# Grouped-query values: the low parts of the probabilities against the high parts of the values alone, in two column groups of 64

## The chip, the cores and the metric

The kernel runs on one core of one Trainium2 chip. The metric is the device time of one execution in microseconds (us), the median of several runs. The core has five engines with instruction queues of their own: TensorE (PE in the profile, with its weight loads apart as PEld), VectorE (DVE), ScalarE (ACT), GpSimd (POOL) and SyncE (SP, which here only issues DMAs).

## The reference, cut to what matters

Two layers of a transformer trunk on 512 latent and 256 context tokens of width 1024. Each layer has a neighbourhood attention and a grouped-query attention beside each other, which share one input projection. The change lies in the grouped-query attention of the latent queries: 8 query heads of width 64, two key/value heads (four query heads share one), 512 queries in four blocks of 128, 768 keys (256 context, 512 latent).

```python
def _attend(q, k, v):
    s = jnp.einsum('bqkgd,btkd->bkgqt', q, k).astype(jnp.float32) * (HEAD_DIM ** -0.5)
    p = jax.nn.softmax(s, axis=-1).astype(v.dtype)
    return jnp.einsum('bkgqt,btkd->bqkgd', p, v)
...
    k_all = jnp.concatenate([ckb, kb], axis=1)
    v_all = jnp.concatenate([cvb, vb], axis=1)
    b_att = _gqa_latent(qb, k_all, v_all)     # _attend for blocks of 128 queries
```

All of it is float32 in the reference.

## The kernel before

To keep float32 precision, the kernel splits operands into a high part and a low part (the rest after rounding), and sums products of the parts. In the projections that makes three matmuls out of one (`mm3`, lines 435 to 437). In the grouped-query attention, the probabilities of a head are turned (transposed) by DMA as two float16 halves: tile `ht` has 4 query blocks x 12 x 128 columns, where entries 0 to 5 of the 12 are the six key tiles of the high part, and 6 to 11 those of the low part (`turned`, lines 841 to 846). The values lie in tile `vb` as float16: for each key tile and key/value head 64 columns of high part beside 64 columns of low part.

`gq_values` (line 1167) computes the output of one head. `divide` first brings the reciprocals of the softmax sums to all partitions (four transposes, L853) and scales the gate `zb` with them (L854). Then 12 matmuls accumulate in one PSUM tile `po` of 128 partitions x 512 queries: for each of the six key tiles, the 128 columns of `vsl(k)` (high and low values) are the stationary operand, and all 512 queries of the probabilities' high part (L1178), then of the low part (L1179), are the moving one. So partitions 0 to 63 of `po` hold the product with the high values, 64 to 127 that with the low values, and `head_out` adds the two halves (L828 copies one on ScalarE, L829 adds the other on VectorE) and multiplies by the gate (L833 on GpSimd).

`pipeline` runs the scores of head h (`gq_scores`: L890 and L891 on PE, L1161 on DVE, the exponential L1162 on ACT, the two halves L841 on ACT and L842 on DVE or POOL, the turn L846) ahead of the values of head h-1, with projection work (`fill`: L435 to L437 on tiles `psf` and `psx`) handed in between. Layer 0 also has context queries (`ctx_scores`, `ctx_values`: L903, L905, L909, L925) and the weights' modulation sums (L297 on DVE, with tile `rawb` loaded by SP). The first projection of the kernel also uses matmuls with 32 stationary columns in four column groups (`ada_part`, L254).

The order of instructions on each engine is set when the kernel is built: a scheduler takes the instructions of all heads, estimates when each can run, and writes one fixed order for each engine. It places matmuls of the scores and of the fill between the matmuls of `gq_values` where it expects them to be ready. In some places the kernel fixes the order itself (`behind`).

Of the kernel before, what the change touches and what calls it, by code (L numbers as in the profile page):

```python
# [72 lines left out]
def hybrid_kernel(es: ExitStack, tc, x, ctx, cvec, w_ada, w_ada0, small, gvec, w_in, w_o_a, w_o_b, w_out,  # L73
                  bias_int, bias_edge, rope, ident_d, out):
    nc = tc.nc
    V, S, G, T = nc.vector, nc.scalar, nc.gpsimd, nc.tensor
# [39 lines left out]
    def psw(n=512, kind="w"):  # L116
        if kind == "w":
            kind = "f" if pm["i"] % pm["n"] == 0 else "x"
            pm["i"] += 1
            if pm["i"] in pm["v_for"]:  # L120
                kind = "v"
        pool, cols = pm[kind]
        return pool.tile([128, cols], F32, tag=kind, name=nm("ps" + kind))[:, :n]
# [471 lines left out]
    def layer(l, hx, nxt, start):  # L595
# [195 lines left out]
        if True:  # L791
# [29 lines left out]
            def head_out(po, e, dst, eng=None, back=None):  # L821

                n = dst.shape[-1]
                m, o = 64 * e, 64 * (1 - e)
                t1 = att["p"].tile([128, 512], F32, tag="ho", name=nm("ho"), bufs=1)
                a = t1[m:m + 64, :n]
                if back is None:
                    S.copy(a, po[o:o + 64, :n])  # L828
                    V.tensor_tensor(a, po[m:m + 64, :n], a, ALU.add)  # L829
                else:  # L830
                    S.activation(a, po[o:o + 64, :n], AF.Copy, scale=back[o:o + 64])
                    V.scalar_tensor_tensor(a, po[m:m + 64, :n], back[m:m + 64], a, ALU.mult, ALU.add)
                (eng or G).tensor_tensor(dst, dst, a, ALU.mult)  # L833
# [14 lines left out]
            def divide(ps, r, e, dst, back):  # L848

                n = r.shape[-1]  # L850
                V.reciprocal(r, r)
                for i in range(n):
                    T.transpose(ps[:, 128 * i:128 * i + 128], r[:, i:i + 1].to_broadcast([128, 128]), ident)  # L853
                V.scalar_tensor_tensor(dst, ps[64 * e:64 * e + 64, :128 * n], back[64 * e:64 * e + 64], dst,  # L854
                                       ALU.mult, ALU.mult)
# [227 lines left out]
            vb = vbig[:, 0:768].bitcast(F16).rearrange("p (t h q d) -> p t h q d", t=6, h=2, q=2)  # L1083
# [83 lines left out]
            def gq_values(h, st):  # L1167
                ht, r = st
                e, kv = h % 2, h // 4

                def vsl(t):
                    return vb[:, t, kv].rearrange("p q d -> p (q d)")
                dst = zb.rearrange("p (f n) -> p f n", f=4)[64 * e:64 * e + 64, h // 2, 0:512]
                divide(psw(512, "t"), r, e, dst, vs[:, 1:2])
                po = psw(512, "t")
                pv = po.rearrange("p (i n) -> p i n", i=4)
                for k in range(6):
                    T.matmul(pv, vsl(k), ht[:, :, k, :], start=k == 0, stop=False)  # L1178
                    T.matmul(pv, vsl(k), ht[:, :, 6 + k, :], start=False, stop=k == 5)  # L1179
                head_out(po, e, dst, V if h == 7 else G)  # L1180
                return vsl

# [12 lines left out]
            def early():  # L1195

                for c in (1, 3):
# [5 lines left out]
                   "junk": vbig[:, 2176:2432].bitcast(BF16)}  # L1203
            bg = gate_steps((1,), Parts(att["p"], own)) if first else []
            pipeline(fill, 8, gq_first, values_of(zb, gq_values, vs[:, 1:2], True), early, bg)
            gq_es.close()

# [322 lines left out]
```

## Time and profile before

| what | value |
|---|---|
| three runs | 1109.35, 1105.3, 1109.29 us |
| median | 1109.29 us |
| span of the profiled execution | 1109.3 us |
| PE busy | 1075.5 us, 97% of the span |
| PE weight loads busy | 879.1 us |
| DVE, ACT, POOL busy | 767.4, 617.1, 473.1 us |
| grouped-query stage of layer 0 | about 375 to 540 us of the span |
| grouped-query stage of layer 1 | about 946 to 1045 us of the span |

The profile shows one execution; its time is its span, since nothing else is shown around it. Busy time of an engine is the time in which at least one of its instructions ran. A matmul's shown duration includes its way through the array, so that several overlap; how fast matmuls follow one another is read from their starts. In the groups, a row gives line, engine, operation, output and inputs by the program's names, shapes and count, then the busy time and the mean duration in ns.

### The profile page before, as it was taken

The numbers are of one execution on the slowest core, as the hardware profiler recorded it, in microseconds if no ns is written. First come the engines' busy times: TensorE is split into PE (matmuls) and PEld (weight loads), VectorE is DVE, ScalarE is ACT, GpSimd is POOL, SyncE is SP. The second block draws the span as 40 slices with busy tenths as digits, with TensorE's granted clock in tenths as the row PEclk, the third lists the DMA queues.
The fourth block names the chain that finished last, engine by engine and source line by source line (L and its number), as shares of the span: only waits on it lengthen the run. The fifth ranks groups of instructions, "written<-read, shape, count | busy, mean of one in ns | idle before, by whom it ended". The sixth has DMA issues, their size and how long they took to land. (4 is left out here: it accounts for less than half of the span.)

```text
span 1109.3 us, 16937 instructions
## 1 busy us (share of the span) xinstructions
PE 1075.5 (97%) x5672; PEld 879.1 (79%) x5672; DVE 767.4 (69%) x1600; ACT 617.1 (56%) x1236; POOL 473.1 (43%) x397
## 2 busy tenths in 40 slices
PE   8999999999999989989999999999999999999998
PEld 5688888788888868767788878888877888777677
DVE  4667889975377487766777785366997665677473
ACT  6454279776433566765330275444899446786430
POOL 1054235555257154463621354232355472564531
PEclk9999999999999999998999999999999999999999
DMA  9455324554543379789633542453565536879642
GB/s 370 146 171 153 90 68 111 128 138 120 169 131 127 100 184 215 166 228 228 213 101 124 157 147 78 140 163 101 134 149 130 156 107 171 199 229 239 188 152 77
DMA packets 236000, 171.79 MB, mean 155 GB/s; under 512 B 160140, under 2 KB 201864, under 8 KB 234248
## 3 DMA queue, kind: packets, MB, share of 16 engines
q1 hardware_dynamic: 228576, 156.31, 51.6%
q0 software_dynamic: 2368, 7.87, 2.1%
q10 hardware_dynamic: 4968, 6.53, 1.8%
q8 instruction: 45, 0.74, 0.3%
q14 instruction: 43, 0.35, 0.1%
HBM read 115.58 MB, written 17.32 MB: 120 GB/s over the span
## 5 line engine op out<-in xcount | busy, mean ns | idle before, releaser
L842 POOL TENSOR_TENSOR h<-p,h 128x256 f16<-128x256 f32 (+2 forms) x104 | 113.6, 1101 | 160.0 <-ACT h L841 117.7
L422 POOL TENSOR_TENSOR wlo<-raw,whi 128x512 fp32r<-128x512 f32 x70 | 98.0, 1406 | 131.6 <-ACT whi L420 98.7
L435 PE MATMUL psf<-hx,whi 128*128 128x512 f32 (+1 forms) x360 | 138.2, 384 | 2.2 <-DVE zt L627 1.2
L436 PE MATMUL psf<-hx,whi 128*128 128x512 f32 (+1 forms) x360 | 136.1, 378 | 0.0
L437 PE MATMUL psf<-hx,wlo 128*128 128x512 f32 (+1 forms) x360 | 136.1, 378 | 0.0
L435 PE MATMUL psx<-whi,hx 128*128 128x512 f32 (+1 forms) x328 | 121.0, 372 | 0.0
L437 PE MATMUL psx<-whi,hx 128*128 128x512 f32 (+1 forms) x328 | 120.0, 367 | 0.0
L420 ACT CAST whi<-raw 128x512 fp32r<-128x512 f32 x136 | 83.2, 620 | 65.5 <-DMA raw<-in_w_in_dram 46.9
L436 PE MATMUL psx<-wlo,hx 128*128 128x512 f32 (+1 forms) x328 | 119.6, 366 | 0.0
L408 POOL TENSOR_TENSOR wlo<-raw,whi 128x512 fp32r<-128x512 f32 x40 | 59.8, 1499 | 117.7 <-ACT whi L405 74.6
L405 ACT CAST whi<-raw 128x512 fp32r<-128x512 f32 x88 | 54.3, 623 | 96.7 <-PE psx L437 34.2
L508 POOL TENSOR_TENSOR ss<-ss,ehalf 128x8 f32<-128x8 f32 (+2 forms) x40 | 63.6, 1593 | 77.2 <-DVE ss L505 72.2
L841 ACT CAST h<-p 128x256 f16<-128x256 f32 (+2 forms) x136 | 81.7, 616 | 5.3 <-DMA ht<-h 1.3
L422 DVE TENSOR_TENSOR wlo<-raw,whi 128x512 fp32r<-128x512 f32 x66 | 65.3, 992 | 25.9 <-ACT whi L420 24.3
L1161 DVE CUSTOM_DVE_ANT_0 p<-pss,vb 128x768 f32<-128x768 f32 x64 | 60.2, 953 | 31.0 <-PE pss L891 28.9
L1162 ACT ACTIVATE p<-pss,mx 128x768 f32<-128x768 f32 x64 | 57.6, 901 | 41.1 <-DVE mx L1161 40.4
L435 PEld LDWEIGHTS psf<-hx,whi 128*128 128x128 f32 x360 | 68.3, 190 | 14.9 <-ACT zt L625 1.9
L437 PEld LDWEIGHTS psf<-hx,wlo 128*128 128x128 f32 x360 | 68.2, 190 | 12.0
L436 PEld LDWEIGHTS psf<-hx,whi 128*128 128x128 f32 x360 | 68.3, 190 | 10.9
L437 PEld LDWEIGHTS psx<-whi,hx 128*128 128x128 f32 x328 | 61.9, 189 | 10.2
L436 PEld LDWEIGHTS psx<-wlo,hx 128*128 128x128 f32 x328 | 62.0, 189 | 9.5
L435 PEld LDWEIGHTS psx<-whi,hx 128*128 128x128 f32 x328 | 61.8, 189 | 9.1 <-issue 0.2
(338 smaller groups left out, 2984.7 us busy)
## 6 DMA issues: line engine op xcount, KB each, us to landing
raw<-in_w_in_dram SPq DMA_DIRECT2D x168, 256.0 KB, 3.0
rawb<-in_w_ada_dram SPq DMA_DIRECT2D x48, 256.0 KB, 2.8
raw<-in_w_out_dram SPq DMA_DIRECT2D x32, 256.0 KB, 2.9
tg<-gs SPq DMA_DIRECT2D x4, 1536.0 KB, 9.9
rawx<-in_w_ada_dram SPq DMA_DIRECT2D x4, 1024.0 KB, 10.3
rawy<-in_w_ada_dram SPq DMA_DIRECT2D x4, 1024.0 KB, 10.3
gs<-zt ACTq DMA_DIRECT2D x16, 256.0 KB, 2.6
raw<-in_w_o_a_dram SPq DMA_DIRECT2D x16, 256.0 KB, 3.1
```

Source lines behind the costliest of these rows:

```text
L405: S.copy(hi[:, :n], raw[:, :n])
L408: e.tensor_tensor(lo[:, :n], raw[:, :n], F(hi[:, :n]), ALU.subtract)
L420: S.copy(hi, raw)
L422: lo_eng(i).tensor_tensor(lo, raw, F(hi), ALU.subtract)
L435: T.matmul(ps, lhs[0], rhs[0], start=first, stop=False)
L436: T.matmul(ps, lhs[0], rhs[1], start=False, stop=False)
L437: T.matmul(ps, lhs[1], rhs[0], start=False, stop=last)
L508: G.tensor_tensor(ss, ss, ehalf[:, :n], ALU.pow)
L841: S.copy(h[:, 0], p[:, :n])
L842: eng.tensor_tensor(h[:, 1], p[:, :n], h[:, 0], ALU.subtract)
L1161: V.tensor_tensor_reduce(p, pss, lift, -1.0, 3e38, ALU.add, ALU.min, mx[:, 0:1])
L1162: S.activation(p, pss, AF.Exp, bias=mx[:, 0:1], accum_out=r[:, i:i + 1])
```

## The change

The high part of the probabilities is multiplied as before, but all six key tiles first. The low part is multiplied by the high values alone (64 stationary columns, `vhi(k)`), and in two matmuls instead of one: the first two query blocks (c = 0) write partitions 0 to 63 of `po`, the other two (c = 1) partitions 64 to 127. Since `head_out` adds the two halves of the partitions for every query, each query receives its low product once. The product of low probabilities and low values is no longer computed.

```diff
+
+                def vhi(t):
+                    return vb[:, t, kv, 0, :]
...
                 for k in range(6):
                     T.matmul(pv, vsl(k), ht[:, :, k, :], start=k == 0, stop=False)
-                    T.matmul(pv, vsl(k), ht[:, :, 6 + k, :], start=False, stop=k == 5)
+                for k in range(6):
+                    for c in range(2):
+                        T.matmul(pv[64 * c:64 * c + 64, 2 * c:2 * c + 2, :], vhi(k), ht[:, 2 * c:2 * c + 2, 6 + k, :],
+                                 start=False, stop=k == 5)
```

In the changed kernel L1181 is the high part (L1178 before) and L1184 the low part (L1179 before); lines 1180 and later have moved down by 6, so that DVE, ACT and POOL keep the lines used here up to 1162.

The scheduler writes another order from the first grouped-query head on. On PE, in the first head's values of layer 0, a score block of the next head (tile `pss`) stands between two products with `vb`. Before:

```order
L1178 MATMUL pst_4512<-ht_4208,vb_3419 128x512
L890 MATMUL pss_4458<-gk_3421,qs_4423 128x512
L891 MATMUL pss_4458<-gk_3421,qs_4423 128x512
L890 MATMUL pss_4458<-gk_3421,qs_4423 128x256
L891 MATMUL pss_4458<-gk_3421,qs_4423 128x256
L1179 LDWEIGHTS vb_3419
L1179 MATMUL pst_4512<-ht_4208,vb_3419 128x512
```

The same place on PE now, where a row of the low part has 64 stationary columns and 256 queries (64x256):

```order
L1181 MATMUL pst_4512<-ht_4208,vb_3419 128x512
L1184 LDWEIGHTS vb_3419
L1184 MATMUL pst_4512<-ht_4208,vb_3419 64x256
L890 MATMUL pss_4458<-gk_3421,qs_4423 128x512
L891 MATMUL pss_4458<-gk_3421,qs_4423 128x512
L890 MATMUL pss_4458<-gk_3421,qs_4423 128x256
L891 MATMUL pss_4458<-gk_3421,qs_4423 128x256
```

The score block has kept its place, and now stands behind the first of the twelve matmuls of the low part, which it parts from the other eleven. Counted over the whole order, the 192 matmuls of the low part stand in 27 unbroken runs. By head, in layer 0: 1+2+9, 4+3+5, 4+5+3, 12, 8+4, 7+3+2, 12, 12; in layer 1: 12, 12, 1+3+8, 12, 12, 12, 12, 12.

On DVE, some rows later in the same head: the reciprocal of the softmax sums (L851), the context scores' maximum (L903, L905), a low half (L842), a modulation sum (L297) and the next head's queries (L884). Before:

```order
L903 TENSOR_REDUCE mx_4494<-pss_4489 128x2
L842 TENSOR_TENSOR h_4467<-p_4463,h_4467 128x768
L297 ISA rawb_4455,asum<-rawb_4455,vb_3419 128x512
L297 ISA asum 128x1
L851 RECIPROCAL r_868_4427<-r_868_4427 128x4
L905 TENSOR_SCALAR mx_4494<-mx_4494 128x2
L884 TENSOR_TENSOR qs_4932<-qb_3734,qs_4932 64x768
```

And now:

```order
L903 TENSOR_REDUCE mx_4494<-pss_4489 128x2
L851 RECIPROCAL r_868_4427<-r_868_4427 128x4
L905 TENSOR_SCALAR mx_4494<-mx_4494 128x2
L842 TENSOR_TENSOR h_4467<-p_4463,h_4467 128x768
L297 ISA rawb_4455,asum<-rawb_4455,vb_3419 128x512
L297 ISA asum 128x1
L854 SCALAR_TENSOR_TENSOR zb_4067<-pst_4765,vb_3419,zb_4067 64x512
L884 TENSOR_TENSOR qs_4944<-qb_3734,qs_4944 64x768
```

The reciprocal and the maximum have moved ahead of the low half and the modulation sum; the next head's queries stay behind them, and behind the scaling of the gate (L854), which has moved ahead of them.

## The prediction

> **What bounds the kernel now.** I read the page's busy table first, then the stretches of the two grouped-query stages, then the groups by line, and last the timeline at the places where the change acts. One row of the page and two of the stretches (length, then busy time and count of PE, PEld, DVE, ACT, POOL, then the granted clock, DMA share and GB/s):
>
> ```profile
> PE 1075.5 (97%) x5672; PEld 879.1 (79%) x5672; DVE 767.4 (69%) x1600; ACT 617.1 (56%) x1236; POOL 473.1 (43%) x397
> 375.00:540.00 165.00, 153.14 (x845) 123.38 (x844) 116.43 (x206) 104.58 (x203) 79.69 (x54) 0.96 0.78 193
> 946.00:1045.00 99.00, 95.89 (x454) 70.45 (x453) 67.37 (x107) 67.49 (x121) 58.24 (x39) 1.00 0.88 220
> ```
>
> PE is the bound in both stages: 153.1 of 165 us, and 95.9 of 99. So what the change takes from PE, or adds to it, counts nearly in full, except in the 12 us and 3 us in which PE waits. Layer 0's clock is 0.96; that comes back below.
>
> Of the changed line, the groups show the count, and the timeline of PE shows the pace at which matmuls follow one another (start, duration):
>
> ```profile
> L1179 PE MATMUL pst<-ht,vb 128*128 128x512 f16 x96 | 36.4, 379 | 0.0
> 490.08 0.38 PE L1178 MATMUL pst<-ht,vb 128*128 128x512 f16 x1 [0.93 <-DVE zb L854]
> ...
> 492.45 0.38 PE L1179 MATMUL pst<-ht,vb 128*128 128x512 f16 x1
> 487.84 0.60 PE L925 MATMUL psv<-vb 128*128 128x256 f16 x4
> L925 PE MATMUL psv<-vb x16: 272/273/283, 403.1 to 526.1; 128*128 128x256 f16 x16
> ```
>
> The twelve matmuls of a head start 2.37/11 = 0.2155 us apart; their 379 ns overlap. With 256 queries in place of 512, four take 0.60 us, of which the last one's 0.273 is latency: (0.60 - 0.273)/3 = 0.109 us apart.
>
> **The change, part by part.** *The old low part* goes: 96 matmuls at 0.2155 us = 20.7 us of PE's time.
>
> *The new low part* is 192 matmuls with 256 queries. What they cost hangs on whether the two column groups run beside each other. This kernel has a case of column groups, the 32-column matmuls of L254 in its first stage. Two bursts of 16 records each in PE's timeline, of 512 and of 256 elements, each between the same neighbours, and the weight loads of the second:
>
> ```profile
> 30.48 0.40 PE L1302 MATMUL psf<-wlo,hx 128*128 128x512 f32 x1
> 30.71 0.39 PE L1304 MATMUL psf<-whi,hx 128*128 128x512 f32 x1
> 31.03 1.06 PE L254 MATMUL pst<-rawy,scol 128*32 128x512 f32 x8
> 31.91 1.04 PE L254 MATMUL pst<-rawx,scol 128*32 128x512 f32 x8
> 32.88 0.50 PE L1301 MATMUL psx<-whi,hx 128*128 128x512 f32 x1
> 33.22 0.40 PE L1302 MATMUL psx<-wlo,hx 128*128 128x512 f32 x1
> ...
> 49.66 0.39 PE L1304 MATMUL psf<-whi,hx 128*128 128x512 f32 x1
> 49.98 1.07 PE L254 MATMUL pst<-rawy,scol 128*32 128x256 f32 x16
> 50.98 0.50 PE L1301 MATMUL psx<-whi,hx 128*128 128x512 f32 x1
> 51.32 0.40 PE L1302 MATMUL psx<-wlo,hx 128*128 128x512 f32 x1
> 49.98 0.59 PEld L254 LDWEIGHTS pst<-rawy,scol 128*32 128x32 f32 x16 [0.35 <-issue]
> ```
>
> By the last row, the loads of the second burst (49.98 to 50.57) lie inside its matmuls (49.98 to 51.05). Sixteen matmuls of 256 elements in 1.07 us, latency included, are too many for one after another: at 0.109 us each they would take over 1.7 us. So column groups do run beside each other, and I take that for two groups of 64 in float16 too: a pair (c = 0 and c = 1) in 0.109 us, where one old matmul took 0.2155.
>
> *Going in and out of column groups* has a price, which the same rows give. From L1304 in front to the second matmul behind (L1302) it is 33.22 - 30.71 = 2.51 us for the long burst and 51.32 - 49.66 = 1.66 for the short one. Doubling the elements costs 0.85, so the short burst streams for 0.85 too. L1304 and L1301 take a slot of 0.23 each (30.48 to 30.71). What is left is 1.66 - 0.46 - 0.85 = 0.35 us per burst in which PE streams nothing: it runs empty, loads weights, and does the same on the way back. With 64 columns the first load is a little longer; I take 0.36.
>
> The Trainium skill ("TensorEngine Tiling (Array Packing)", section Tiling Modes, key properties) says that changing the tiling mode drains TensorE, which agrees with the 0.35 us, for which it has no figure. Its section Overview promises up to twice the speed where at most 64 columns are used. By that speedup alone, without the drain, the estimate would be half of the old low part saved, some 10 us, and 1099 us.
>
> *The number of bursts* comes from the order: 27 in 16 heads, not 16, since score blocks and fill are placed between the parts. An odd run leaves one half without its partner. Rounded up by run, the pairs' slots are 52 in layer 0 (17 runs) and 49 in layer 1 (10 runs). So:
>
> - layer 0: before 48 x 0.2155 = 10.3 us; now 52 x 0.109 + 17 x 0.36 = 5.7 + 6.1 = 11.8: **+1.4**
> - layer 1: before 10.3; now 49 x 0.109 + 10 x 0.36 = 5.3 + 3.6 = 8.9: **-1.4**
>
> The sum is 0.0. A whole run of 12 saves 1.29 - 0.65 - 0.36 = 0.28 us; a head cut in three loses 0.5. Bounds of this term: if every switch fell into a wait of PE, -9.7 (27 x 0.36); if the groups did not run together, +9.7 (below).
>
> *What costs nothing*: 96 more matmuls and 96 more loads to issue (L254's 32 instructions issue within its 1.07 us); no new data, since `vhi` is a slice of `vb`; no DMA, and no other engine's work changes. The order of all high parts before the low ones adds no wait: the first high matmul needed all four query blocks of `ht` already.
>
> *What is moved*: the scheduler's order on every engine from the first head on. Here the two long waits of PE in layer 0's stage matter. The first, with its waits (us in all, times, longest), the DVE rows, and POOL beside them:
>
> ```profile
> PE pst L853 <- DVE mx L905: 2.9, 1, 2.9
> 406.77 4.61 DVE L297 CUSTOM_DVE_ANT_0 rawb<-rawb,vb 128x512 f32<-128x512 f32 x1
> 411.31 0.16 DVE L851 RECIPROCAL r<-r 128x4 f32<-128x4 f32 x1
> 411.56 0.95 DVE L884 TENSOR_TENSOR qs<-qb,qs 64x768 fp32r<-64x768 f32 x1
> 405.46 2.55 POOL L833 TENSOR_TENSOR zb<-zb,ho 64x512 f32<-64x512 f32 x1 [4.01 <-DVE ho L829]
> 409.58 1.25 POOL L422 TENSOR_TENSOR wlo<-raw,whi 128x512 fp32r<-128x512 f32 x1
> L297 DVE CUSTOM_DVE_ANT_0 rawb<-rawb,vb x8: 679/684/4611, 387.1 to 458.2; 128x512 f32<-128x512 f32 x8
> 410.70:417.60 6.90, 6.07 (x17) 0.51 0.61 155
> ```
>
> L297 takes 0.684 us as a rule and 4.61 here: it ends just after POOL's chain (409.58 + 1.25 = 410.83). Behind it stand the reciprocal for L853 and the next queries (L884). The last row is the stretch after: the clock granted to PE was 0.51 for 6.9 us, which loses another 3.4. The second wait is built alike:
>
> ```profile
> 493.94 3.60 DVE L842 TENSOR_TENSOR h<-p,h 128x768 f16<-128x768 f32 x1 [0.32 <-ACT h L841]
> 489.54 7.18 POOL L672 TENSOR_TENSOR gal<-za,gah 128x768 fp32r<-128x768 f32 x4
> 500.22 0.79 PE L890 MATMUL pss<-gk,qs 128*128 128x512 f32 x1 [2.71 <-ACT p L1162]
> 499.50:506.30 6.80, 6.08 (x23) 0.50 1.07 277
> ```
>
> A wait of this kind costs 2.9 + 3.4 = 6.3 us, and there are two. The new order moves the reciprocal and L905 ahead of the first L297, so PE gets its L853 some 5 us earlier; but L884, which the next scores need, is still behind L297, now with L854 ahead of it as well. So I expect that wait again, some tenths longer, with its 0.45 us of L853 already done: nothing gained. Of the later heads I can't say which DVE operation will meet which POOL chain; I take two such waits again.
>
> Sum: span 1109.3 (the profiled execution shows no time beside it, and the median of the runs is 1109.29) + 1.4 - 1.4 + 0.0, and some tenths for the longer path at the first wait: **1109.5 us**, no change. 0.5% of it, 5.5 us, is about what a measurement of this kernel can tell from no change.
>
> **The rivals.** *One wait fewer.* If the new order lets one of the two DVE operations run clear of POOL's chain, 6.3 us go: 1109.3 - 6.3 = 1103.0. For it: L297 is at 0.684 us in most of its 8 cases, so the meeting is rare and hangs on tenths. Against it: L884 stays behind the same L297. Switches that fall into PE's 12 idle us would push the same way.
>
> *One wait more.* The same meeting once more, in a head that the new order has shifted: 1109.3 + 6.3 = 1115.6. For it: layer 0 holds 1.4 us more PE work, in pieces that cut the scores apart. Against it: in layer 1, with the same code, no such wait occurred (clock 1.00).
>
> *The groups don't run beside each other* in this form. Then 192 matmuls at 0.109 us take 20.9, as before, and the 27 switches come on top: 1109.3 + 0.2 + 9.7 = 1119.2. It decides from the first pair: starts 0.1 us apart and not 0.01. For it: no row here shows 64 columns or float16 in column groups. Against it: the burst of L254. The same time would come out if the weights of a group could not be loaded while the other's matmul runs, as each slot would then be longer by about a load. The Trainium skill ("TensorE: Matmul & The Clock Gate", Part 3, the mechanism) says that a weight load overlaps with running matmuls only in other row groups. These pairs share all rows, so by that rule this rival would hold; the trace speaks against it, with L254's loads inside its matmuls on the same rows.
>
> **How the numbers follow.** Sum as worked out 0.47 (1109.5, own range 1104.5 to 1114.5); one wait fewer 0.25 (1103.0); one wait more 0.16 (1115.6); groups apart 0.12 (1119.2). So faster by over 0.5% 0.25, within 0.5% 0.47, slower 0.28. The range reaches from 1101.5, a wait fewer with a few switches hidden, to 1118.5, just short of the last rival, which it leaves out with the deeper half of the first.
>
> **What would show it.** In the changed profile: L1184 starts in pairs some 0.01 us apart and 0.11 us from pair to pair; from the last matmul ahead of a run of 12 to the second behind it about 0.2155 + 0.65 + 0.36 + 0.23 = 1.46 us; PE's stage in layer 1 shorter by about 1.4 us; in layer 0 two stretches at half clock, each after a DVE operation of 3 us or more beside POOL. Pairs 0.1 apart, a switch much under or over 0.36, or another number of half-clock stretches would make it wrong.

## The result, and the profile after

The changed kernel took 1114.76 us (median of 6 runs, 1113.92 to 1118.43) against 1108.02 for the kernel before it (6 runs, 1105.3 to 1109.35): a ratio of 1.0069, with a 95% interval of 1.0052 to 1.0086. A second measurement gave 1116.21 against 1109.02, 1.0061 (1.0047 to 1.0074). So the change costs 0.6 to 0.7%, about 7 us. That lies inside the predicted range, but the likeliest forecast, no change at 1109.5, did not come true; the number is that of the rival "one wait more" (1115.6), and the runs show another cause for it.

The execution profiled took 1117.34 us, of which the span is 1115.6. The busy row of TensorE and layer 0's stretch of the prediction, now 1 us later:

```profile
PE 1076.5 (96%) x5768; PEld 876.8 (79%) x5768; DVE 765.4 (69%) x1600; ACT 617.3 (55%) x1236; POOL 463.5 (42%) x397
376.00:541.00 165.00, 148.74 (x870) 117.64 (x869) 114.94 (x204) 103.61 (x201) 78.35 (x54) 0.97 0.81 192
```

In 165 us of layer 0's stage, PE is busy 148.7 where it was 153.1, and the stage got no shorter. Most of that difference is not work saved: 2.7 us are gate matmuls that have left the stage (below), and over the whole span PE is busy as long as before (1076.5 against 1075.5).

**The new matmuls do what the prediction says.** The view of one line, and one whole run of twelve in TensorE's timeline (start, duration):

```profile
L1184 PEld LDWEIGHTS <-vb x192: 106/110/155, 399.8 to 1046.5; 128*64 128x64 f16 x192
L1184 PE MATMUL pst<-ht,vb x192: 272/273/409, 399.8 to 1046.6; 128*64 128x256 f16 x192
470.97 1.47 PE L1181 MATMUL pst<-ht,vb 128*128 128x512 f16 x6
472.37 0.85 PE L1184 MATMUL pst<-ht,vb 128*64 128x256 f16 x12
473.15 0.50 PE L890 MATMUL pss<-gk,qs 128*128 128x512 f32 x1
473.49 0.40 PE L891 MATMUL pss<-gk,qs 128*128 128x512 f32 x1
504.02 0.36 PEld L1184 LDWEIGHTS <-vb 128*64 128x64 f16 x7 [0.42 <-issue]
504.02 0.62 PE L1184 MATMUL pst<-ht,vb 128*64 128x256 f16 x7
```

Twelve matmuls in 0.85 us, of which the last one's 0.273 is latency. In the single records the two of a pair start 3 to 4 ns apart and the pairs 0.109 us (the first step is 0.134). By the last two rows, seven weight loads of 64 columns lie inside the matmuls of a run.

**Where the 6.3 us of span came from.** Landmarks that both kernels have, from TensorE's timelines of the two profiles:

| from, to | before | after | difference |
|---|---|---|---|
| start to the first grouped-query score of layer 0 | 375.75 | 376.76 | +1.0 |
| to layer 0's last value matmul | 162.48 | 163.85 | +1.4 |
| to the first matmul of its output projection | 44.88 | 45.18 | +0.3 |
| to the last of it that reads `mh` | 69.19 | 71.79 | +2.6 |
| to layer 1's first neighbourhood score | 123.34 | 126.43 | +3.1 |
| to its first grouped-query score | 148.18 | 148.54 | +0.4 |
| to its first output projection matmul | 135.24 | 134.76 | -0.5 |
| to the end | 50.18 | 48.21 | -2.0 |

The first and the last row say little of the change. The first lies ahead of what was changed, and its half-clock loss was 3.4 us in after against 1.7 in before; the last is 48.2 or 50.2 us in kernels of either order (48.2 in e4 and e12, which keep the old one).

Two rows need a closer look. The first is layer 0's stage. Its end, in TensorE's timeline of before and then of after (the first and the last of 12 gate matmuls, and the last head's values):

```profile
532.73 0.50 PE L435 MATMUL psf<-gah,whi 128*128 128x512 f32 x1 [0.17 <-DVE tg L707]
...
535.40 0.39 PE L437 MATMUL psf<-gah,wlo 128*128 128x512 f32 x1
535.86 0.38 PE L1178 MATMUL pst<-ht,vb 128*128 128x512 f16 x1
```

```profile
533.94 0.28 PE L437 MATMUL psf<-gah,wlo 128*128 128x256 f32 x1
537.27 0.59 PE L1181 MATMUL pst<-ht,vb 128*128 128x512 f16 x1 [3.05 <-issue]
539.92 0.96 PE L1184 MATMUL pst<-ht,vb 128*64 128x256 f16 x12
540.81 0.50 PE L435 MATMUL psf<-gah,whi 128*128 128x512 f32 x1
...
543.46 0.39 PE L437 MATMUL psf<-gah,wlo 128*128 128x512 f32 x1
```

The block of 12 gate matmuls (2.7 us) stood ahead of the last head's values; in the new order it stands behind them, and TensorE is idle for 3.05 us in its place. So 2.7 us of work have left the stage, which is 1.4 us longer all the same: with equal work it lost 4.1 in this profile, and 2.2 in that of e1, the same kernel again, where the stage took 162.0. (The +2.6 two rows further down is that work: 12 gate matmuls more behind the first output projection matmul.)

The idle time ends when the last turn (DMA) of that head lands, at 537.18 in after, where the values start at 537.27; in before it lands at 535.73 and they start at 535.86. Its time from issue to landing, in before and then in after:

```profile
ht<-h SPq DMA_TRANSPOSE x1, 3.2
```

```profile
ht<-h SPq DMA_TRANSPOSE x1, 4.8
```

From 531 to 534.6 us the packets of that DMA queue took 69.9% of the 16 engines' time in before, and all of it in after (106.6% by the profile's count). So two things make the 3.05 us: the work that had covered the wait is gone, and the turn takes 1.6 us longer, in a fuller queue. It takes 4.8 to 6.0 us in the four kernels with the new order in this stage (after, e1, e3, e6), and 3.2 in before, e5 and e9 to e12; in e2, e4, e7 and e8, with the old order, it takes 4.9 to 5.2.

The second is the +3.1 after the output projection. What TensorE's matmuls and loads waited for from layer 0's last values to layer 1's neighbourhood scores (us in all, times, longest), in before:

```profile
PE pst L343 <- DVE y L334: 1.7, 1, 1.7
PE psx L436 <- DVE wlo L408: 0.2, 1, 0.2
PEld psx L436 <- DVE wlo L408: 0.5, 1, 0.5
```

and in after:

```profile
PE psx L436 <- DVE wlo L408: 1.5, 3, 0.9
PE pst L343 <- ACT half L346: 0.8, 2, 0.6
PEld psx L436 <- DVE wlo L408: 2.8, 3, 1.3
PEld pst L343 <- ACT half L346: 2.1, 3, 1.1
```

VectorE's timeline there in after, with the wait in brackets, and what TensorE did:

```profile
653.82 0.43 DVE L350 CAST hx<-half 128x512 fp32r<-128x512 f32 x1 [1.65 <-ACT half L346]
...
656.16 1.45 DVE L351 TENSOR_TENSOR hx<-half,hx 128x512 fp32r<-128x512 f32 x1
657.53 1.77 DVE L1260 TENSOR_TENSOR xt<-xt,t 128x512 f32<-128x512 f32 x1
659.23 0.68 DVE L408 TENSOR_TENSOR wlo<-raw,whi 128x512 fp32r<-128x512 f32 x1
659.96 0.50 PE L436 MATMUL psx<-wlo,hx 128*128 128x512 f32 x1 [0.86 <-DVE wlo L408]
```

The low half of the weights (`wlo`, L408) stands on VectorE behind operations that wait for ScalarE, which waits for transposes of TensorE, which itself waits for `wlo`. In before VectorE had no such idle time from 646 to 660 us. Nothing here belongs to the values: the order of another stage, 100 us later, has changed.

### The profile page after: what moved, and what is told of

The parts are those of the page before. It is cut to its first block, busy times and chain, and to the rows that moved or that the text cites. A ratio compares the mean times of both kernels' runs of the same rounds, so it can differ in the third digit from the quotient of the medians.

```text
span 1115.6 us, 17125 instructions
## 1 busy us (share of the span) xinstructions
PE 1076.5 (96%) x5768; PEld 876.8 (79%) x5768; DVE 765.4 (69%) x1600; ACT 617.3 (55%) x1236; POOL 463.5 (42%) x397
## 5 line engine op out<-in xcount | busy, mean ns | idle before, releaser
L842 POOL TENSOR_TENSOR h<-p,h 128x256 f16<-128x256 f32 (+2 forms) x104 | 110.9, 1075 | 171.5 <-ACT h L841 121.1
L422 POOL TENSOR_TENSOR wlo<-raw,whi 128x512 fp32r<-128x512 f32 x70 | 97.4, 1397 | 121.4 <-ACT whi L420 90.2
L408 POOL TENSOR_TENSOR wlo<-raw,whi 128x512 fp32r<-128x512 f32 x40 | 53.5, 1341 | 129.0 <-ACT whi L405 89.9
L422 DVE TENSOR_TENSOR wlo<-raw,whi 128x512 fp32r<-128x512 f32 x66 | 61.0, 928 | 37.2 <-ACT whi L420 36.9
```

The source lines that it names most:

```text
L408: e.tensor_tensor(lo[:, :n], raw[:, :n], F(hi[:, :n]), ALU.subtract)
L422: lo_eng(i).tensor_tensor(lo, raw, F(hi), ALU.subtract)
L842: eng.tensor_tensor(h[:, 1], p[:, :n], h[:, 0], ALU.subtract)
```

## The experiments

All orders below are laid down in the same way: the order that the scheduler made of one kernel is recorded per engine and given to another kernel, by tying each instruction to the one that it must follow on its own engine, with no semaphore:

```python
for a, b in zip(seq, seq[1:]):
    tc.add_manual_dep(b, a.name, mybir.DependencyInfo(
        mybir.DependencyClass.NoSync, mybir.DependencyReason.DATA), reason="a given order")
```

"Old order" is that of the kernel before, "new order" that of the changed one. The list makes line numbers larger (L1178 of before is L1413 in most of them, L890 is L1124 or L1125). In all tables "rest" is the mean span less the half-clock loss, (1 - granted clock) x span, over the timed runs; of before it is 1100.7 to 1101.0, with 6.5 to 6.8 of loss.

| run | median us | ratio to before (95%) | half-clock loss | rest |
|---|---|---|---|---|
| e1 changed kernel again | 1116.21 | 1.0061 (1.0047 to 1.0074) | 7.6 | 1107.0 |
| e2 old order, new matmuls | 1111.99 | 1.0025 (1.0012 to 1.0037) | 9.2 | 1101.1 |
| e3 new order, old matmuls | 1115.77 | 1.0056 (1.0043 to 1.0068) | 6.9 | 1107.1 |
| e4 old order, one run per head | 1111.47 | 1.0022 (1.0013 to 1.0032) | 8.7 | 1100.9 |
| e5 before, new order after the values | 1116.64 | 1.0058 (1.0039 to 1.0076) | 6.9 | 1107.2 |
| e6 after, old order after the values | 1112.62 | 1.0034 (1.0018 to 1.0050) | 5.4 | 1106.0 |
| e7 old order, new matmuls in layer 1 | 1107.74 | 0.9984 (0.9973 to 0.9995) | 6.7 | 1099.2 |
| e8 no low part in layer 0 | 1112.15 | 1.0028 (1.0017 to 1.0038) | 11.4 | 1099.2 |
| e9 as e5, first half | 1113.90 | 1.0039 (1.0027 to 1.0052) | 6.6 | 1105.6 |
| e10 as e5, second half | 1112.64 | 1.0029 (1.0015 to 1.0044) | 7.2 | 1103.7 |
| e11 as e10, VectorE old | 1124.56 | 1.0139 (1.0118 to 1.0161) | 10.3 | 1113.4 |
| e12 no low part in layer 1 | 1106.61 | 0.9974 (0.9961 to 0.9986) | 7.3 | 1097.9 |

**Order or matmuls?** Four kernels of one batch separate the two. e1 is the changed kernel once more:

> The changed kernel once more, on the chip of the next three. In its profile a run of 12 takes 1.42 us from the matmul ahead to the second behind, so 0.33 us per switch; the sum over 101 pair slots and 27 runs is 11.0 + 8.9 = 19.9 us of PE against 20.7 before, -0.8. Both theories: 1.005 to 1.009 of before.

e2 has the changed kernel's code in the old order, where the low parts fall into 21 runs:

> The new matmuls in the old order: every instruction of every engine is chained in the order that the scheduler wrote for the kernel before; of a head's 12 places on PE the first six hold the high parts, the last six a pair of low parts each. 21 unbroken runs, 96 pair slots. Theory A (the new order makes the waits, the matmuls themselves gain a little): 96 x 0.109 + 21 x 0.33 - 20.7 = -3.3 us, so about 1105, 0.997 of before. Theory B (the column groups themselves cost it: drains and late head outputs make the waits in whatever order): as slow as the changed kernel, +6 to +8 us, 1.006.

e3 is the reverse, the matmuls of before in the new order, so that all six high parts come first (against before):

```diff
                 for k in range(6):
                     T.matmul(pv, vsl(k), ht[:, :, k, :], start=k == 0, stop=False)
+                for k in range(6):
                     T.matmul(pv, vsl(k), ht[:, :, 6 + k, :], start=False, stop=k == 5)
```

> The old matmuls (128 columns, 512 queries, high and low values) in the new order on every engine: each low part stands where the changed kernel has the first half of its pair. Theory A: the new order's waits without the gain of the pairs, +7.6 + 0.8 = about +8 us, 1.007 to 1.008 of before. Theory B: as before, 1.000.

e4 is e2 with all twelve low matmuls of a head in the last of its places, 16 runs:

> As the new matmuls in the old order, but all twelve low matmuls of a head stand together at the last of its places, so that a head goes in and out of column groups once: 16 runs. Theory A: 96 x 0.109 + 16 x 0.33 - 20.7 = -4.9 us, about 1103, 0.9955 of before, and 1.6 us under the kernel with 21 runs. Theory B: +4 us or more, since 16 drains remain.

The new order costs 6.2 us with the old matmuls (e3, 6.4 by the rest); with the new ones it is 4.2 by the medians (e1 less e2) and 5.9 by the rest. The new matmuls in the old order should have gained 3 to 5 us of TensorE's time; they gained nothing by the rest (1101.1 and 1100.9 against 1100.7) and lost 2.1 to 2.6 us to half-clock time. Neither theory had that: A expected e2 and e4 to gain, and B no cost of the order in e3.

**Where does the order cost it?** e5 and e6 exchange the order only from layer 0's last value matmul to the end of the merge, in opposite directions:

> The kernel before, old matmuls and old order on every engine, except for the stretch from layer 0's last value matmul to the end of its output projection and merge (some 583 to 707 us of the profile of before), where every engine takes the order of the changed kernel. Theory M (the new order in that stretch, not the value matmuls and not their stage, costs the 6 us): +5 to +6.5 us, 1.0045 to 1.006. Rival V (the cost lies in the order of the values' stage itself, or in what that stage hands on): 1.000. Rival C (the half-clock time alone makes the difference): 1.000 with the span less its half-clock loss as before.

> The mirror of it: the changed kernel, new matmuls and new order, except for the same stretch, where every engine takes the order of the kernel before. Theory M: the 6 us are gone, 1.000 to 1.002 against before (1.0061 for the whole changed kernel). Rival V: still 1.005 to 1.007.

Theory M alone would have brought e6 back to 1.000 to 1.002; it came to 1.0034, so it holds only in part. A mixed order also has a seam, which e9 and e10 show by halving e5's stretch:

> The kernel before with old matmuls and old order, the new order only from layer 0's last value matmul to the first rows of its output projection (up to some 605 us). In the profile of e5 TensorE waits 2.57 us there for the transfer of ct, since the gate matmuls that stood before it now stand behind. If the two halves of the 6 us add up: +2.5 us, 1.002 to 1.0025. If the first half is made up later: 1.000. If it carries all: 1.0055.

> The same with the new order only in the second part, the rest of the output projection and the merge (some 605 to 707 us). In the profile of e5 TensorE waits there 1.03 + 0.79 + 0.61 + 0.38 us in its four longest gaps (VectorE's wlo of L408 and the transposes of the merge, L343), and its distance to layer 1's neighbourhood scores is 3.9 us longer: +3.5 to +4 us, 1.003 to 1.0035. If that half is innocent: 1.000.

The first rows of VectorE's order that e10 changes (line numbers of before; L297 sums modulation weights, L1252 and L1254 write the residual, L408 splits weights):

```diff
 L297
 L1254
+L408
 L297
+L1252
+L408
+L1254
+L408
 L297
-L408
 L297
-L408
-L1252
```

e10 costs 1.0029, 3.2 us, with the wait of the changed kernel (0.86 us there as here):

```profile
650.70 0.50 PE L670 MATMUL psx<-wlo,hx 128*128 128x512 f32 x1 [0.86 <-DVE wlo L642]
652.76 0.66 PE L577 MATMUL pst<-ident,y 128*128 128x128 f32 x4 [0.62 <-ACT half L580]
657.18 0.50 PE L670 MATMUL psx<-wlo,hx 128*128 128x512 f32 x1 [0.43 <-DVE wlo L642]
```

and its distance from output projection to neighbourhood scores is 126.41, that of after (126.43). e6 takes it out of the changed kernel: there the distance is 123.34 again. In every profile with the old order in this half it is 123.3 to 123.4, and in all five with the new one on every engine 126.4 to 127.4. So some 3.1 us of the change's cost lie in this half. The timed runs of e6 say so less firmly: the ratio falls from e1's 1.0061 to 1.0034, some 3 us, but the two intervals overlap, and by the rest the cost falls only from 6.3 us to 5.0. e9's 4.3 us are different. They come from the seam:

```profile
537.04 0.61 PE L1159 MATMUL psv<-ct,vb 128*128 128x256 f16 x4 [2.50 <-DMA ct<-h]
619.70 0.50 PE L670 MATMUL psx<-wlo,mh 128*128 128x512 f32 x1 [2.08 <-DVE wlo L642]
```

Neither wait is in the changed kernel, where 12 gate matmuls stand ahead of that `psv`. So e5's 1.0058, inside theory M's range, is in part the seam's. What the changed kernel has in their place is the 3.05 us at 537.27, which e1 and e3 have too (3.2 and 3.7 us) and e6 keeps (3.03). That would account for most of the 3.8 us that are left in e6, but it was not tried by itself.

> As e10, but VectorE alone keeps the old order; TensorE, ScalarE and GpSimd have the new one there. If VectorE's order makes those waits: 1.000 to 1.001. If TensorE's or ScalarE's new order makes them: 1.003 to 1.0035 as e10. If a VectorE that no longer matches the others stalls them all: over 1.004.

e11 came out by its third line, and far beyond it: 1.0139.

```profile
641.93 1.97 PE L577 MATMUL pst<-ident,y 128*128 128x128 f32 x8 [4.33 <-DVE y L568]
659.12 0.50 PE L670 MATMUL psx<-wlo,hx 128*128 128x512 f32 x1 [2.74 <-DVE wlo L642]
670.09 0.50 PE L670 MATMUL psx<-wlo,hx 128*128 128x512 f32 x1 [3.84 <-DVE wlo L642]
```

Three waits of 10.9 us in all: an engine's order fits those of the others, or costs more than either whole order. So "VectorE's new order is the cause" is not shown; it is the order of all four together.

**Does TensorE bound the stage?** e8 and e12 leave the low parts' 48 matmuls out, in layer 0 or in layer 1, all in the old order, so that the outputs lack them. This is e8; e12 has `if not first`:

```diff
-                for k in range(6):
-                    T.matmul(pv, vsl(k), ht[:, :, k, :], start=k == 0, stop=False)
-                    T.matmul(pv, vsl(k), ht[:, :, 6 + k, :], start=False, stop=k == 5)
+                if first:
+                    for k in range(6):
+                        T.matmul(pv, vsl(k), ht[:, :, k, :], start=k == 0, stop=k == 5)
+                else:
...
```

> The kernel before, old order, with the 48 matmuls of the low parts in layer 0 left out (the output lacks them). If layer 0's values stage is bound by TensorE: 48 x 0.2155 = 10.3 us less, 0.9907. If TensorE's saved time turns into waits there (theory W, as the first four runs suggest): 0 to -4 us, 0.9965 to 1.000; a little over 1.000 if the longer waits bring one half-clock stretch more (1.7 to 3.4 us).

> The kernel before, old order, with the 48 matmuls of the low parts left out in layer 1 instead of layer 0 (the output lacks them). If layer 1's values stage is bound by TensorE (theory W): 48 x 0.2155 = 10.3 us of work gone, -8 to -10 us, 0.991 to 0.993. If it swallows them as layer 0 did (e8, 1.0028): 0.998 to 1.003.

Layer 0's stage, first score to last values, in before and in e8:

```profile
375.75:538.23 162.48, 150.62 (x828) 121.12 (x827) 115.74 (x205) 103.33 (x200) 79.69 (x54) 0.96 0.78 193
375.20:538.39 163.19, 143.04 (x781) 117.83 (x780) 119.27 (x205) 103.35 (x200) 79.27 (x54) 0.95 0.79 193
```

With 10.3 us of TensorE's work gone, the stage is as long as before and the kernel 2.5 us slower by the medians; by the rest it gained 1.8 us, and the half-clock loss rose from 6.5 to 11.4.

One event stands in the profiles of e2, e4, e7 and e8 and in no other. On VectorE a `wlo` operation (L422 of before, L657 here) takes 5.88 us beside GpSimd's own `wlo`, TensorE waits 2.9 us for the reciprocal behind it, and a half-clock stretch follows. e7 and e12 run the same instructions in the same order in layer 0; this is the operation in e7 and then in e12:

```profile
524.15 5.88 DVE L657 TENSOR_TENSOR wlo<-raw,whi 128x512 fp32r<-128x512 f32 x1
```

```profile
523.11 0.68 DVE L657 TENSOR_TENSOR wlo<-raw,whi 128x512 fp32r<-128x512 f32 x1
```

It looks like the meeting of VectorE and GpSimd that the prediction describes, and it came in one profile and not in another of the same order. It may be where e2, e4 and e8 lost what they saved in layer 0; no run tests that.

Layer 1's stage in before and in e12:

```profile
923.82:1044.51 120.69, 117.22 (x554) 88.11 (x553) 79.89 (x128) 83.55 (x149) 66.81 (x44) 1.00 0.85 210
919.18:1039.13 119.95, 109.62 (x506) 84.29 (x505) 80.26 (x128) 83.03 (x149) 66.26 (x44) 0.99 0.84 211
```

There the kernel gains 2.8 us of 10.3, where theory W had expected 8 to 10. The waits of TensorE in that stretch grew instead, in before and in e12:

```profile
PE psf L435 <- DVE tg L707: 0.8, 2, 0.5
PE pss L890 <- ACT p L1162: 0.5, 1, 0.5
```

```profile
PE pss L1125 <- ACT p L1397: 5.0, 6, 1.9
PE psf L670 <- DVE tg L942: 3.3, 2, 1.7
```

The scores wait until the exponentials of an earlier block (ACT, `p`) have freed their buffer, and the gate for VectorE's `tg`. A TensorE that is busy 97% of a stretch waited for other engines as soon as it had 9% less to do. VectorE is at 66% there, ScalarE at 69%, and the DMA share is 0.85. The waits point at the round trip from score to exponential to value, in this order; that it sets the pace is not shown. The chain of work that ended last in e12 also runs through a transfer of output weights (`raw`, 9.4 us at 982), and no run took transfers away. Whether a new order would turn the freed time into gain stays open too.

**A version that beats both.** e7 takes the new matmuls in layer 1 alone, one run per head, in the old order:

```diff
+                if first:
+                    for k in range(6):
+                        T.matmul(pv, vsl(k), ht[:, :, k, :], start=k == 0, stop=False)
+                        T.matmul(pv, vsl(k), ht[:, :, 6 + k, :], start=False, stop=k == 5)
+                else:
...
+                            T.matmul(pv[64 * c:64 * c + 64, 2 * c:2 * c + 2, :], vhi(k), ht[:, 2 * c:2 * c + 2, 6 + k, :],
+                                     start=False, stop=k == 5)
```

> The old order on every engine; old matmuls in layer 0, the new ones in layer 1 alone, each head's twelve in one run (8 heads: 8 x 0.31 us less of TensorE by my own sum, 2.4 us). If layer 1's values stage is bound by TensorE: -2 to -2.5 us, 0.9977 to 0.9982. If its saved time turns into waits as layer 0's did: 1.000. If the new form adds half-clock time there: up to 1.003.

0.9984, that is 1.8 us less (0.6 to 3.0), from 2.4 us of TensorE's time. It is small, but zero lies outside its interval, and its half-clock loss (6.7) is that of before.

## Why the prediction was right or wrong

- *The base, 1109.3 us*: the span was taken for the time. In every later run the time is 1.7 to 1.9 us more than the span, and six runs of before have the median 1108.02. This shifts the forecast by about 1 us and explains nothing of the 7.
- *Old low part, 20.7 us of TensorE*: not in question.
- *A pair in 0.109 us*: right, 0.109.
- *0.36 us for going in and out of column groups*: nearly right. From the last matmul ahead of a run of 12 to the second behind, 1.42 us were measured where 1.46 were predicted, so the price is 0.33 (in the one run that began at half clock it is 1.79 in place of 1.42). The Trainium skill ("TensorEngine Tiling (Array Packing)", Tiling Modes) says that the switch drains TensorE, without a figure; the 0.33 us fit that.
- *27 runs, sum 0.0*: 101 x 0.109 + 27 x 0.33 = 19.9 against 20.7, so -0.8. A size slightly off.
- *Groups apart (0.12)*: refuted by the first pair, 3 to 4 ns apart. The rule that it was weighed with (the Trainium skill, "TensorE: Matmul & The Clock Gate", Part 3, the mechanism: loads overlap only with matmuls in other row groups) does not hold in these words for these column groups: seven loads take their 0.36 us within the matmuls on the same rows.
- *PE is the bound, so what is taken from it "counts nearly in full"*: **wrong, the first step that failed.** I read 153.1 of 165 us busy as a bound. e8 and e12 took 10.3 us off and got 1.8 and 2.9 back by the rest. The -0.8 could not have been seen either way, but the rivals' prices were built on this too.
- *What is moved*: **the second step that failed, and the one that made the 7 us.** I followed the order through the two long waits of layer 0's stage and stopped there. Neither came as described. In place of the first, TensorE waits 1.8 us for L853, ahead of the long VectorE operation (now L905, 3.60 us, in place of L297's 4.61), and 1.95 us behind it, where the next scores wait for the context queries' exponentials (L909), which need L905; they start before L884. The second, behind L842, is gone, and waits of 2.0 us stand at 452 and 515 us:

```profile
407.61 0.16 DVE L851 RECIPROCAL r<-r 128x4 f32<-128x4 f32 x1
407.72 3.60 DVE L905 TENSOR_SCALAR mx<-mx 128x2 f32<-128x2 f32 x1
412.10 0.68 DVE L297 CUSTOM_DVE_ANT_0 rawb<-rawb,vb 128x512 f32<-128x512 f32 x1
413.60 0.95 DVE L884 TENSOR_TENSOR qs<-qb,qs 64x768 fp32r<-64x768 f32 x1
```

But the order was also new in two places that the prediction does not name: the 12 gate matmuls at the end of layer 0's stage, which had covered the last head's wait, and VectorE's splits in the merge. TensorE's wait in the one is 3.05 us, and the distance over the other grew by 3.1; both came with the old matmuls too (e3). That the second costs its 3.1 us is shown; that the first makes up the rest is argued. I wrote "from the first head on" and costed one place.
- *Two half-clock stretches of 6.8 us in layer 0*: after shows three of 3.4 (1.7 us lost in each, 5.1 against 6.8), in other places:

```profile
413.90:417.30 3.40, 3.40 (x10) 2.75 (x9) 3.21 (x7) 0.39 (x2) 2.21 (x2) 0.50 1.10 243
454.90:458.30 3.40, 3.40 (x18) 3.40 (x18) 0.89 (x3) 3.19 (x7) 2.74 (x3) 0.50 0.32 104
536.80:540.20 3.40, 2.93 (x10) 0.99 (x12) 0.46 (x1) 0.62 (x1) 1.76 (x2) 0.50 0.85 220
```

  The prediction named another number of stretches as a sign that it was wrong, and three is such a number. But the number changes from one execution to the next: e1, the same kernel, has a single stretch in layer 0's stage, and e9, e10 and e12, with the old order there, have two of 3.4 behind the same two waits as before. So the 3.4 us of loss in the price of a wait belonged to one profile.

- *One wait more, 1115.6*: the right number by another mechanism. The wait was new, but it was a cover that had gone and a slower turn, not a VectorE operation beside GpSimd, and half of the cost lay in another stage. Nor did half-clock time add to it, as that rival's price has it: the mean loss was 6.7 and 7.6 us in the two measurements of the changed kernel, 6.6 in before. That the range holds the result is luck: its sum has nothing for either place.
- *Layer 1 shorter by 1.4*: by the landmarks 0.5. A single profile can't tell this from nothing; e7, with layer 1 alone, gained 1.8 where 2.4 were due.

## What to carry to other kernels

Where a scheduler sets the order, an edit is two changes: give the new code the old order, and the old code the new one, before a time is put down to the instructions. Read the whole difference of the orders on every engine to the end of the program, and above all which work has left its place ahead of a wait. And a busy share of 93 or 97% does not make an engine the bound: leave the work out once and see what comes back.

## What the runs showed of the hardware

- Two matmuls in column groups of 64 start 3 to 4 ns apart on the same rows, and pairs 0.109 us apart, half of a full matmul's 0.2155, with weight loads inside; going in and out of the mode costs 0.33 us of streaming.
- Less work for TensorE in layer 0 brought more half-clock time: the mean loss per run went from 6.5 us to 11.4 with 48 matmuls fewer in layer 0, and to 9.2 and 8.7 with the new matmuls in the old order. Less work in layer 1 did not (6.7 in e7; 7.3 in e12, against 6.8). In these profiles half-clock time comes in stretches of 3.4 or 6.8 us, but for the last, which the end of the span cuts; those of layer 0's stage stand in or behind waits of TensorE of 1 to 4 us, though not every such wait brings one. So a saving that ends as a wait is not free here.
- The same instructions in layer 0's stage, in the same order, took 155.7 to 160.8 us without the half-clock loss in seven profiles. Differences of a stage by 2 us need the timed runs.
- One VectorE operation (`wlo`, 128x512) took 0.68 us in e12 and 5.88 in e7, in the same order, in e7 beside a chain of GpSimd operations.
